# MoBA's output projection in a hybrid decoder layer: y_b kept as pairs of leading bits and rest, products of 512 and 256 columns in place of three of 256, two halves added per block

## The chip, the cores and the metric

The kernel runs on one core of one Trainium2 chip. The metric is the device time of one execution in microseconds (us), the median of a few runs. The profile shown is of one execution of its own.

## The reference, cut to what matters

One decoder layer for 256 tokens of width 1024, all in float32. Two token mixers read the same projection of x, each is projected once more, the two are mixed by gates, and a feed-forward net follows:

```python
proj = jnp.einsum('bsd,dn->bsn', x, w_in)
hq, hf, hi, hg, mq, mk, mv, gate_logits = jnp.split(proj, offsets, axis=-1)
y_a = rms_norm(hgrn2_mixer(hq, hf, hi, lb), hgrn_norm_w) * silu(hg)     # 256 x 1024
y_b = moba_attention(rope(mq), rope(mk), mv)                            # 256 x 1024, 8 heads of 128
z_a = jnp.einsum('bsc,cd->bsd', y_a, w_branch_a)
z_b = jnp.einsum('bsc,cd->bsd', y_b, w_branch_b)                        # the product of this case
g_a, g_b = jnp.split(jax.nn.sigmoid(gate_logits + b_gate), 2, axis=-1)
mixed = jnp.einsum('bsc,cd->bsd', g_a * z_a + g_b * z_b, w_out)
x = layer_norm(DN_ALPHA * x + mixed, ln1_w, ln1_b)
h_gate, h_up = jnp.split(jnp.einsum('bsd,df->bsf', x, w_ffn_in), 2, axis=-1)
y = jnp.einsum('bsf,fd->bsd', silu(h_gate) * h_up, w_ffn_down)
return layer_norm(DN_ALPHA * x + y, ln2_w, ln2_b)
```

With 256 tokens there is one MoBA block, so the attention is plain causal attention over the 256 tokens.

## The kernel before, in words

**Two parts for each operand.** Every float32 operand of a large product is split into its leading bits (`h`, a copy into the type float32r) and the rest (`l`, the difference), `split` at L209. A product a·w is made of three matmuls: h·h, l·h and h·l. Two ways of issuing them matter here:

- `feat_pair` (L298) with `feat_steps` (L349) makes a block of 256 output channels. For each half `f` of 128 channels and each of the eight slices `k` of 128 inputs it issues three matmuls of 256 columns (the tokens): `wh`·`ah` (L353), `wh`·`al` (L354) and `wl`·`ah` (L355). All of them add up in one PSUM tile of 128x512, which holds both halves.
- `wide_pair` (L306) needs the activation as a `Pair` (L166): leading bits and rest of a slice lie side by side in one SBUF tile. For each `f` and `k` it issues one matmul of 512 columns, `wh`·(`ah`,`al`) (L315), and one of 256, `wl`·`ah` (L316). Each half `f` has a PSUM tile (a bank of 128x512) of its own, with the h·h and h·l sums in its first 256 columns and the l part in the last 256. `wide_sum` (L321) then adds the two: for each `f` a ScalarE copy of the last 256 columns to SBUF (L325) and a VectorE add of the first 256 (L326).

The gates `gb` and `ga`, the projection `za` of the other mixer and the feed-forward blocks `fg` and `fu` go by `wide_pair`; the queries and keys and `zb`, the projection of this case, go by `feat_pair`.

**Weights.** `stage` (L217) brings one tile of 128x2048 float32 (1 MB) at a time: SyncE's queue loads it into `raw` (three buffers), ScalarE copies it to `wh` (L236), VectorE subtracts to get `wl` (L238). `wh` and `wl` have four buffers each, so a tile is staged when TensorE has finished with the tile four before. `fetch` (L258) stages up to three tiles ahead of the one that it hands out. Some loads are tied to a transfer on GpSimd's queue that adds up weight blocks in HBM (`sum_weights`, L247); the tiles of `zb` and of `w_out` are not.

**The stretch around the change.** The attention heads (`moba_head`, L696) write their output `po` with `split` into `ybh` and `ybl` (L726), one slice of 256 tokens per head; the eight heads run beside the projections `za0` to `za3` (L754). Then four blocks `zb0` to `zb3` follow (L769): `feat_pair`, the product with the gate on VectorE straight from PSUM (L772), the sum with the other branch (L773), and the split into `mTh` and `mTl` (L774). Slices 2j and 2j+1 of `mTh` and `mTl` come from block j. The products with `w_out` follow (L885 to L917): for the first 128 tokens four groups q = 0 to 3 (`rows_pass`, L783), group q reading slices 2q and 2q+1, 12 matmuls of 512 columns each, in the order `mTh`·`wh`, `mTh`·`wl`, `mTl`·`wh` (L793 to L795); then the layer norm of the first tokens (`norm1(0)`) on VectorE beside the four groups of the second 128 tokens.

**Order.** A scheduler at build time orders the instructions of each engine by its own model of their durations, except inside the stretches marked `manual_schedule`, where TensorE, VectorE and ScalarE follow the order of the program; the products with `w_out` and what follows up to L917 are such a stretch. Each engine then works through its list in that order.

**Memory.** PSUM has eight banks: the pool `mm` (four, used by `za`, `zb` and the attention scores among others) and `aux` (four). At L764 the pools of the scan and the attention (`klp`, `hd2`) are closed, and the pools `late` and `gate` are opened in their place. `kept` is a tile of 128x1024 float32 in `gate`, made at L922 and first written in the feed-forward stage.

Of the kernel before, what the change touches and what calls it, by code (L numbers as in the profile page):

```python
# [10 lines left out]
F32 = mybir.dt.float32  # L11
F32R = mybir.dt.float32r
# [5 lines left out]
P = 128  # L18
T = 256
# [3 lines left out]
H = 8  # L23
# [121 lines left out]
def hybrid_layer_kernel(ctx: ExitStack, tc, x, xw, vecs, wts, ln1_w, ln1_b, ln2_w, ln2_b, consts, out):  # L145
    nc = tc.nc
# [10 lines left out]
    mm = pool("mm", 4, space=PSUM)  # L157
    aux = pool("aux", 4, space=PSUM)

    def slot(name, dt=F32):  # L160
        return big.tile([P, 2048], dt, tag="s8", name=name)

    def r32(ap):
        return ap.bitcast(F32)
# [44 lines left out]
    def split(dst_h, dst_l, src):  # L209
        nc.scalar.copy(dst_h, src)  # L210
        nc.vector.tensor_sub(dst_l, src, r32(dst_h))
# [46 lines left out]
    def fetch(ahead=LOOKAHEAD):  # L258
        while state["next"] < len(loads) and len(ready) < 1 + ahead:
            list(stage())  # L260
        return ready.pop(0)
# [36 lines left out]
    def feat_pair(name, ah=None, al=None, p=mm):  # L298
        ah, al = (xTh, xTl) if ah is None else (ah, al)
        wh, wl = fetch()  # L300
        ps = p.tile([P, 2, T], F32, tag="mm" if p is mm else "aux", name=name)
        for f in range(2):
            feat_steps(ps[:, f, :], wh, wl, f, ah, al, range(KC))
        return ps

    def wide_pair(name, p, tag, a):  # L306


        wh, wl = fetch()
        pss = []  # L310
        for f in range(2):
            ps = p.tile([P, 2, T], F32, tag=tag, name=f"{name}{f}")
            wcol = slice(f * P, (f + 1) * P)
            for k in range(KC):
                nc.tensor.matmul(ps, wh[:, k, wcol], a.both(k), start=(k == 0), stop=False)  # L315
                nc.tensor.matmul(ps[:, 0, :], wl[:, k, wcol], a[0, k, slice(0, T)],  # L316
                                 start=False, stop=(k == KC - 1))
            pss.append(ps)
        return pss

    def wide_sum(pss, dst):  # L321


        for f, z in enumerate(pss):
            nc.scalar.copy(dst[f], z[:, 1, :])  # L325
            nc.vector.tensor_add(dst[f], z[:, 0, :], dst[f])  # L326
# [22 lines left out]
    def feat_steps(ps, wh, wl, f, ah, al, ks, k0=0):  # L349
        wcol = slice(f * P, (f + 1) * P)  # L350
        for k in ks:
            kk = k0 + k
            nc.tensor.matmul(ps, wh[:, k, wcol], ah[:, kk, :], start=(kk == 0), stop=False)  # L353
            nc.tensor.matmul(ps, wh[:, k, wcol], al[:, kk, :], start=False, stop=False)  # L354
            nc.tensor.matmul(ps, wl[:, k, wcol], ah[:, kk, :], start=False, stop=(kk == KC - 1))  # L355
# [81 lines left out]
    for j in range(4):  # L437
        ps = feat_pair(f"hq{j}")
# [5 lines left out]
        for f in range(2):  # L444
            h = 2 * j + f
# [206 lines left out]
    gb = slot("gb").rearrange("p (c t) -> p c t", c=KC)  # L652
# [15 lines left out]
    qT = slot("qT").rearrange("p (h t) -> p h t", h=H)  # L668
    kT = slot("kT").rearrange("p (h t) -> p h t", h=H)
    mv = slot("mv").rearrange("p (t d) -> p t d", t=NT)  # L670
    ybh = slot("ybh", F32R).rearrange("p (h t) -> p h t", h=H)
    ybl = slot("ybl", F32R).rearrange("p (h t) -> p h t", h=H)

    def rope_pair(nm, dst, j, p=mm):
        ps = feat_pair(f"m{nm}{j}", p=p)
# [15 lines left out]
    def spared(i):  # L691
        if not spares:
            spares.append(klp.tile([P, 2, 3 * P], F32, tag="kl", name="ms"))
        return spares[0][:, i, :]

    def moba_head(h):  # L696
        ps = mm.tile([P, 3 * P], F32, tag="mm", name=f"s{h}")
        nc.tensor.matmul(ps[:, 0:P], qT[:, h, 0:P], kT[:, h, 0:P], start=True, stop=True)
        nc.tensor.matmul(ps[:, P:3 * P], qT[:, h, P:T], kT[:, h, :], start=True, stop=True)
        s = hd2.tile([P, 3 * P], F32, tag="ms", name=f"ms{h}") if h % 4 < 2 else spared(h % 4 - 2)  # L700
        st = sm.tile([P, 8], F32, tag="st", bufs=4, name=f"st{h}")
        nc.vector.tensor_tensor(s, ps, causal, op=ALU.add)
        nc.vector.tensor_reduce(st[:, 2:3], s[:, 0:P], axis=mybir.AxisListType.X, op=ALU.max, negate=True)
        nc.vector.tensor_reduce(st[:, 3:4], s[:, P:3 * P], axis=mybir.AxisListType.X, op=ALU.max, negate=True)
        p = s
        nc.scalar.activation(p[:, 0:P], s[:, 0:P], AF.Exp, bias=st[:, 2:3], accum_out=st[:, 4:5])
        nc.scalar.activation(p[:, P:3 * P], s[:, P:3 * P], AF.Exp, bias=st[:, 3:4], accum_out=st[:, 5:6])
        nc.vector.reciprocal(st[:, 6:8], st[:, 4:6])
        nc.scalar.mul(p[:, 0:P], p[:, 0:P], st[:, 6:7])
        nc.scalar.mul(p[:, P:3 * P], p[:, P:3 * P], st[:, 7:8])  # L710
        yield
        pt = aux.tile([P, 3 * P], F32, tag="aux", name=f"pt{h}")
        for b in range(3):
            nc.tensor.transpose(pt[:, b * P:(b + 1) * P], p[:, b * P:(b + 1) * P], ident)
        pT = hd2.tile([P, P], F32, tag="pT", name=f"pT{h}")
        both = hd2.tile([P, 2, T], F32R, tag="sg", bufs=3, name=f"pTp{h}")
        pTh, pTl = both[:, 0, :], both[:, 1, :]
        split(pTh, pTl, pt[:, 0:T])
        nc.scalar.copy(pT, pt[:, T:3 * P])
        hd = slice(h * P, (h + 1) * P)  # L720
        po = aux.tile([P, T], F32, tag="aux", name=f"po{h}")
        nc.tensor.matmul(po, mvh[:, hd], pTh, start=True, stop=False)
        nc.tensor.matmul(po, mvl[:, hd], pTh, start=False, stop=False)
        nc.tensor.matmul(po, mvh[:, hd], pTl, start=False, stop=False)
        nc.tensor.matmul(po[:, P:T], mv[:, 1, hd], pT, start=False, stop=True)
        split(ybh[:, h, :], ybl[:, h, :], po)  # L726
        yield

    def moba_heads():
        heads = [moba_head(h) for h in range(H)]  # L730
        next(heads[0])
        for i in range(H):
            if i < H - 1:
                next(heads[i + 1])
            next(heads[i])
            yield
# [17 lines left out]
    for j in range(4):  # L754
        side.step()
        cs = slice(2 * j, 2 * j + 2)
        if j in PROJECTIONS:
            z = hd2.tile([P, 2, T], F32, tag="sg", bufs=3, name=f"za{j}s")
            wide_sum(wide_pair(f"za{j}", mm, "mm", yP[0]), [z[:, f, :] for f in range(2)])
        else:  # L760
            z = feat_pair(f"za{j}", yah[0], yal[0])
# [4 lines left out]
    gate = pool("gate", 1)  # L766
    mTh = slot("mTh", F32R).rearrange("p (k t) -> p k t", k=KC)
    mTl = slot("mTl", F32R).rearrange("p (k t) -> p k t", k=KC)
    for j in range(4):  # L769
        ps = feat_pair(f"zb{j}", ybh, ybl)  # L770
        cs = slice(2 * j, 2 * j + 2)
        nc.vector.tensor_mul(gb[:, cs, :], ps, gb[:, cs, :])  # L772
        nc.vector.tensor_add(ga[:, cs, :], ga[:, cs, :], gb[:, cs, :])  # L773
        split(mTh[:, cs, :], mTl[:, cs, :], ga[:, cs, :])  # L774

# [143 lines left out]
    e[1][1].transpose()  # L919


    kept = gate.tile([P, 2, 512], F32, tag="kept", name="kept")  # L922
    unit = lambda z: z.rearrange("p (i k t) -> p i k t", i=4, k=KQ // 2)
    spare = []

# [79 lines left out]
    p, f, g = kept[:, 0, :], kept[:, 1, :], room[:, 0, :, :].rearrange("p f t -> p (f t)")  # L1005
# [60 lines left out]
```

## Time and profile before

| | us |
|---|---|
| median of 3 runs | 492.84 |
| the runs | 492.49, 492.84, 805.31 |
| span of the profiled execution | 491.3 |
| median less span | 1.5 |
| TensorE busy in the span | 482.9 (98%) |
| VectorE busy | 396.2 (81%) |
| ScalarE busy | 315.6 (64%) |

The profile gives no device time of its own for the profiled execution, only its span, from the first to the last instruction; 1.5 us is what the median has beside it. PE is TensorE, PEld its weight loads, DVE is VectorE, ACT is ScalarE, POOL is GpSimd, SP is SyncE. A row of the timeline gives start, duration, engine, line, operation, output and input, count, and in brackets how long the engine had been idle and on what it had waited; rows that follow one another directly and are alike are merged into one with a count. L12 is line 12 of the kernel. The duration of a matmul is its time from start to modelled end; one starts before the one ahead of it has ended.

### The profile page before, as it was taken

The page shows a single profiled execution, that of the slowest core. Times are in us where ns is not written, and L with a number is a line of the kernel's source. Part 1 is how long each engine was busy: PE and PEld are TensorE (multiplying, and loading weights), DVE is VectorE, ACT ScalarE, POOL GpSimd, SP SyncE. Part 2 cuts the span into 40 slices and gives each one's busy share as a digit, 9 for nine tenths or more (in the row PEclk, how much of TensorE's full clock was granted, in tenths as well). Part 3 has the DMA queues.
Part 4 walks back from the last instruction along what each step waited for, and adds up shares of the span by engine and source line. Part 5 has one row for each costly group of instructions (what it writes and reads, how often), then busy time and mean ns, then how long its engine had stood idle before and what let it go on. Part 6 is the DMA issues. An engine that isn't in the chain of part 4 may idle for free.

```text
span 491.3 us, 7536 instructions
## 1 busy us (share of the span) xinstructions
PE 482.9 (98%) x2980; PEld 434.0 (88%) x2980; DVE 396.2 (81%) x490; ACT 315.6 (64%) x446; POOL 66.0 (13%) x89
## 2 busy tenths in 40 slices
PE   9999999999999999999999999999999999999994
PEld 9999888888888999999989988888888888898883
DVE  4888899999879869999773999555886779589947
ACT  6797677655879869789762555444565656587700
POOL 2305150530000010010010000001213010000001
PEclk9999999999999999999999999999999999999998
DMA  8879899999996988669776466049999999999702
GB/s 315 371 263 448 273 294 339 316 356 300 343 330 248 318 300 301 229 228 338 255 268 248 177 257 233 18 176 407 286 307 354 317 310 308 297 361 387 257 0 85
DMA packets 25106, 137.79 MB, mean 280 GB/s; under 512 B 2416, under 2 KB 2544, under 8 KB 13424
## 3 DMA queue, kind: packets, MB, share of 16 engines
q1 hardware_dynamic: 15264, 100.63, 53.2%
q0 software_dynamic: 9808, 36.70, 29.0%
q8 instruction: 23, 0.38, 0.3%
q14 instruction: 11, 0.09, 0.0%
HBM read 136.27 MB, written 34.60 MB: 348 GB/s over the span
## 4 chain that ended last, share of the span: by engine, by line
PE 95%; DVE 2%; DMA 2%; issue 0%; ACT 0%; DVEq 0%
PE fu L315 7%; PE fg L315 7%; PE fg L316 3%; PE fu L316 3%; PE gb L315 3%; PE za L315 3%; PE wd L999 2%; PE wd L1000 2%; PE wd L1001 2%; DMA raw<-in_wts_dram 2%; PE sc L514 2%; PE hf L383 2%; PE ga L315 2%; PE hf L384 2%; PE mk L355 2%; PE zb L355 2%
## 5 line engine op out<-in xcount | busy, mean ns | idle before, releaser
L238 DVE TENSOR_TENSOR wl<-raw,wh 128x2048 fp32r<-128x2048 f32 x89 | 203.0, 2289 | 54.0 <-ACT wh L236 53.5
L236 ACT CAST wh<-raw 128x2048 fp32r<-128x2048 f32 x89 | 169.8, 1916 | 73.9 <-PE fg L315 17.6
L315 PE MATMUL fg<-x1p,wh 128*128 128x512 f32 x144 | 50.5, 394 | 0.0
L315 PE MATMUL fu<-x1p,wh 128*128 128x512 f32 x144 | 50.4, 394 | 0.0
L254 POOL TENSOR_TENSOR mark<-ticks 128x1 f32<-128x1 f32 x32 | 24.4, 762 | 180.8 <-DVE ticks L253 159.9
L316 PE MATMUL fg<-x1p,wl 128*128 128x256 f32 x144 | 40.0, 277 | 0.0
L316 PE MATMUL fu<-x1p,wl 128*128 128x256 f32 x144 | 39.9, 277 | 0.0
L315 PEld LDWEIGHTS fu<-x1p,wh 128*128 128x128 f32 x144 | 27.0, 187 | 6.2
L315 PEld LDWEIGHTS fg<-x1p,wh 128*128 128x128 f32 x144 | 27.0, 187 | 6.1
L316 PEld LDWEIGHTS fg<-x1p,wl 128*128 128x128 f32 x144 | 27.0, 188 | 0.1
L316 PEld LDWEIGHTS fu<-x1p,wl 128*128 128x128 f32 x144 | 27.0, 188 | 0.0
L315 PE MATMUL za<-yP,wh 128*128 128x512 f32 x64 | 23.6, 407 | 0.0
L315 PE MATMUL gb<-xP,wh 128*128 128x512 f32 x64 | 22.7, 397 | 0.0
L315 PE MATMUL ga<-xP,wh 128*128 128x512 f32 x64 | 22.6, 396 | 0.0
L256 POOL DMA_DIRECT2D u<-in_wts_dram x24 | 19.7, 827 | 9.7 <-DMA u<-in_wts_dram 7.3
L353 PE MATMUL mq<-xP,wh 128*128 128x256 f32 x64 | 18.6, 291 | 0.0
L354 PE MATMUL mk<-xP,wh 128*128 128x256 f32 x64 | 18.4, 288 | 0.0
L353 PE MATMUL mk<-xP,wh 128*128 128x256 f32 x64 | 18.3, 285 | 0.0
L316 PE MATMUL za<-yP,wl 128*128 128x256 f32 x64 | 18.3, 285 | 0.0
L355 PE MATMUL mq<-xP,wl 128*128 128x256 f32 x64 | 18.2, 284 | 0.0
L355 PE MATMUL mk<-xP,wl 128*128 128x256 f32 x64 | 18.1, 283 | 0.0
L353 PE MATMUL hq<-xP,wh 128*128 128x256 f32 x64 | 18.1, 283 | 0.0
(338 smaller groups left out, 1388.3 us busy)
## 6 DMA issues: line engine op xcount, KB each, us to landing
raw<-in_wts_dram SPq DMA_DIRECT2D x73, 1024.0 KB, 6.3
raw<-u SPq DMA_DIRECT2D x16, 1024.0 KB, 6.7
u<-in_wts_dram POOLq DMA_DIRECT2D x8, 1024.0 KB, 20.5
u<-u POOLq DMA_DIRECT2D x8, 1024.0 KB, 18.2
first<-in_xw_dram SPq DMA_DIRECT2D x6, 640.0 KB, 9.3
xr<-in_x_dram POOLq DMA_DIRECT2D x1, 1024.0 KB, 5.2
wb<-in_ln_w_dram POOLq DMA_DIRECT2D x2, 512.0 KB, 6.6
wb<-in_ln_b_dram POOLq DMA_DIRECT2D x2, 512.0 KB, 7.9
```

The costliest lines, as they stand in the source:

```text
L236: nc.scalar.copy(h[:, ks, :], raw[:, ks, :])
L238: eng.tensor_sub(l[:, ks, :], raw[:, ks, :], r32(h[:, ks, :]))
L254: tc.keep_in_program_order(nc.gpsimd.tensor_tensor(mark, tick, tick, op=ALU.add))
L256: tc.keep_in_program_order(nc.gpsimd.dma_start(source(dst), source(src), **more))
L315: nc.tensor.matmul(ps, wh[:, k, wcol], a.both(k), start=(k == 0), stop=False)
L316: nc.tensor.matmul(ps[:, 0, :], wl[:, k, wcol], a[0, k, slice(0, T)], start=False, stop=(k == KC - 1))
L353: nc.tensor.matmul(ps, wh[:, k, wcol], ah[:, kk, :], start=(kk == 0), stop=False)
L354: nc.tensor.matmul(ps, wh[:, k, wcol], al[:, kk, :], start=False, stop=False)
L355: nc.tensor.matmul(ps, wl[:, k, wcol], ah[:, kk, :], start=False, stop=(kk == KC - 1))
L383: nc.tensor.matmul(pss[f], wh[:, wcol], xTh[:, k, :], start=(k == 0), stop=False)
L384: nc.tensor.matmul(pss[f], wh[:, wcol], xTl[:, k, :], start=False, stop=False)
L514: nc.tensor.matmul(ps[:, a, :], KL[:, h, :], later(Qt, n, h, 1), start=True, stop=True)
```

## The change

`ybh` and `ybl` become the two halves of a `Pair`, so that a head's leading bits and rest lie side by side. The blocks `zb0` to `zb3` are made by `wide_pair`, and `wide_sum` puts the sum of the two halves into one of two halves of `kept`, from which the product with the gate now reads. For that, `kept` is made ahead of the loop and no longer at L922. Weights, their order and the rest of the kernel stay.

```diff
-    ybh = slot("ybh", F32R).rearrange("p (h t) -> p h t", h=H)
-    ybl = slot("ybl", F32R).rearrange("p (h t) -> p h t", h=H)
+    yb = Pair("yb")
+    ybh, ybl = Part(yb, 0), Part(yb, 1)
...
-        split(ybh[:, h, :], ybl[:, h, :], po)
+        split(ybh[:, h, slice(0, T)], ybl[:, h, slice(0, T)], po)
...
+    kept = gate.tile([P, 2, 512], F32, tag="kept", name="kept")
     for j in range(4):
-        ps = feat_pair(f"zb{j}", ybh, ybl)
+        z = kept[:, j % 2, :].rearrange("p (f t) -> p f t", f=2)
+        wide_sum(wide_pair(f"zb{j}", mm, "mm", yb), [z[:, f, :] for f in range(2)])
         cs = slice(2 * j, 2 * j + 2)
-        nc.vector.tensor_mul(gb[:, cs, :], ps, gb[:, cs, :])
+        nc.vector.tensor_mul(gb[:, cs, :], z, gb[:, cs, :])
         nc.vector.tensor_add(ga[:, cs, :], ga[:, cs, :], gb[:, cs, :])
         split(mTh[:, cs, :], mTl[:, cs, :], ga[:, cs, :])
...
-    kept = gate.tile([P, 2, 512], F32, tag="kept", name="kept")
     unit = lambda z: z.rearrange("p (i k t) -> p i k t", i=4, k=KQ // 2)
```

## The prediction

> **What bounds the kernel now.** I read the page first: span, busy shares, chain.
>
> ```profile
> span 491.3 us, 7536 instructions
> ...
> PE 482.9 (98%) x2980; PEld 434.0 (88%) x2980; DVE 396.2 (81%) x490; ACT 315.6 (64%) x446; POOL 66.0 (13%) x89
> ...
> PE 95%; DVE 2%; DMA 2%; issue 0%; ACT 0%; DVEq 0%
> ```
>
> TensorE sets the end: 95% of the chain that ended last is its work. So the question is how much TensorE time the change takes out, and whether the work it puts on VectorE and ScalarE makes TensorE wait. For both I read stretches: first the busy time of each engine in windows around the change (columns: PE, PEld, DVE, ACT, POOL, granted clock, DMA share, GB/s).
>
> ```profile
> 75.00:140.00 65.00, 64.91 (x377) 56.63 (x377) 62.17 (x80) 43.49 (x53) 12.43 (x15) 1.00 1.02 315
> ...
> 259.00:282.61 23.61, 23.61 (x200) 23.61 (x198) 15.65 (x16) 9.31 (x8) 0.00 (x0) 1.00 0.53 203
> ...
> 264.57:270.09 5.52, 5.52 (x48) 5.52 (x47) 0.00 (x2) 0.12 (x1) 0.00 (x0) 1.00 0.45 184
> 270.09:288.18 18.09, 18.09 (x131) 17.13 (x130) 16.66 (x17) 12.09 (x10) 0.00 (x0) 1.00 0.49 178
> ```
>
> The blocks zb0 to zb3 take 23.61 us (second row), TensorE without a gap, clock full. In the 18.09 us that begin with the product for zb0, VectorE is busy for 16.66, so it has 1.43 us left; before that it does nothing for 5.5 us. The first row, where the gates are made by `wide_pair`, is kept for later.
>
> **TensorE's term.** A matmul's duration isn't its price, since starts overlap. The price is the distance of starts. In the timeline, TensorE alone, an unbroken run of zb:
>
> ```profile
> 273.25 0.28 PE L353 MATMUL zb<-ybh,wh 128*128 128x256 f32 x1
> ...
> 282.49 0.28 PE L355 MATMUL zb<-ybh,wl 128*128 128x256 f32 x1
> 282.61 0.40 PE L793 MATMUL wo<-wh,mTh 128*128 128x512 f32 x1
> ```
>
> From 273.25 to 282.61 there are 26 groups of three, 78 matmuls: 9.36 us, 0.120 us each, 0.360 us for a half and a slice. The same for `wide_pair` from the gate gb, an unbroken run of 23 pairs:
>
> ```profile
> 89.82 0.40 PE L315 MATMUL gb<-xP,wh 128*128 128x512 f32 x1
> 90.05 0.28 PE L316 MATMUL gb<-xP,wl 128*128 128x256 f32 x1
> ...
> 97.80 0.39 PE L315 MATMUL gb<-xP,wh 128*128 128x512 f32 x1
> ```
>
> 7.98 us for 23 pairs is 0.347 us for a half and a slice: 0.23 for the 512 columns, 0.117 for the 256. The change removes 192 matmuls of 256 columns and issues 64 of 512 and 64 of 256, with 64 fewer weight loads. The columns streamed are the same. 64 × (0.360 − 0.347) = **0.8 us less** on TensorE.
>
> [...]
>
> **What is added.** For each of the eight halves one ScalarE copy and one VectorE add, as za has them (duration in ns, least/median/most):
>
> ```profile
> L315 PE MATMUL za<-yP,wh x64: 390/395/582, 230.4 to 258.6; 128*128 128x512 f32 x64
> L316 PE MATMUL za<-yP,wl x64: 274/280/368, 230.7 to 258.9; 128*128 128x256 f32 x64
> L325 ACT COPY za0s<-za x2: 393/398/403, 240.1 to 240.4; 128x256 f32<-128x256 f32 x2
> ...
> L326 DVE TENSOR_TENSOR za0s<-za,za0s x2: 415/415/415, 242.6 to 242.9; 128x256 f32<-128x256 f32 x2
> ```
>
> ```profile
> 242.61 0.75 DVE L326 TENSOR_TENSOR za0s<-za,za0s 128x256 f32<-128x256 f32 x2
> ```
>
> ScalarE: 8 × 0.40 = 3.2 us at most, in a stretch where it is busy 9.3 of 23.6 us. VectorE: 8 × 0.415 = 3.3 us, or 2.7 us if they run back to back: the two in the timeline's row take 0.75 us together, so the second adds 0.33. The product with the gate now reads SBUF and not PSUM; elementwise operations of 128x512 on VectorE take 0.68 to 0.69 us in either case (the products and sums of zb in the next fence), so I put that at nothing.
>
> Does this reach TensorE? VectorE's list in the stretch, the part that matters:
>
> ```profile
> 263.89 0.68 DVE L762 TENSOR_TENSOR ga<-za3s,ga 128x512 f32<-128x512 f32 x1
> 270.09 0.69 DVE L772 TENSOR_TENSOR gb<-zb,gb 128x512 f32<-128x512 f32 x1 [5.52 <-PE zb L355]
> 270.82 0.69 DVE L773 TENSOR_TENSOR ga<-ga,gb 128x512 f32<-128x512 f32 x1
> ...
> 281.12 0.69 DVE L773 TENSOR_TENSOR ga<-ga,gb 128x512 f32<-128x512 f32 x1
> 281.73 0.68 DVE L211 TENSOR_TENSOR mTl<-ga,mTh 128x512 fp32r<-128x512 f32 x1
> 282.81 0.69 DVE L772 TENSOR_TENSOR gb<-zb,gb 128x512 f32<-128x512 f32 x1 [0.40 <-PE zb L355]
> 283.54 0.69 DVE L773 TENSOR_TENSOR ga<-ga,gb 128x512 f32<-128x512 f32 x1
> 284.68 2.29 DVE L238 TENSOR_TENSOR wl<-raw,wh 128x2048 fp32r<-128x2048 f32 x1 [0.45 <-ACT wh L236]
> 286.89 1.29 DVE L211 TENSOR_TENSOR mTl<-ga,mTh 128x512 fp32r<-128x512 f32 x2
> 288.09 4.49 DVE L238 TENSOR_TENSOR wl<-raw,wh 128x2048 fp32r<-128x2048 f32 x2
> 292.50 0.68 DVE L804 SCALAR_TENSOR_TENSOR x<-xr,wo 128x512 f32<-128x512 f32 x1
> ```
>
> The first `mTl` of the pair at 286.89 is that of zb2; it ends near 287.6. It stands behind the last w_out tile's `wl`, which itself waits for zb3 to free its `wh` buffer. On TensorE, group q = 2 of the products with w_out needs it here (282.61 + 24 matmuls is the group's start, its third matmul the first reader):
>
> ```profile
> 288.53 0.39 PE L795 MATMUL wo<-wh,mTl 128*128 128x512 f32 x1
> ```
>
> So zb2's rest has 0.9 us to spare, and after the change TensorE wants it 0.8 us earlier, at 287.7. The 5.5 idle us of VectorE before 270.09 don't help if zb0 again ends near 270 (zb0 is held there because its last slice, that of head 7, comes late in the scheduler's order). Then all eight adds fall into the 18.09 us with 1.43 to spare. **Lower bound of the wait: none**, if the scheduler puts zb2's `mTl` ahead of that `wl` of 2.2 us, or zb0 comes earlier. **Upper bound**: 8 × 0.415 = 3.3 us late with none of the 1.43 us used, so 287.6 + 3.3 − 287.7 = 3.2 us. With the same order and the spare used: 2.7 − 1.4 = 1.3 us late, a wait of 1.2 us. I take **0.4 us**, nearer the lower end, because of the first window above: there, with `wide_sum` in the list, VectorE is busy 62.17 of 65 us, as full as here, and TensorE still has 64.91 of 65.
>
> Other edits. The longer chain behind zb3 (a copy of 0.40 and an add of 0.42) is covered: its `mTl` ends at 288.2 and group q = 3 starts 36 matmuls after 282.61, near 290.8; if that cover goes, it costs those 0.8 us. `norm1(0)` at 292.50 follows VectorE's list; what it makes is wanted by the early feed-forward product:
>
> ```profile
> 301.15 2.29 DVE L238 TENSOR_TENSOR wl<-raw,wh 128x2048 fp32r<-128x2048 f32 x1 [0.42 <-ACT wh L236]
> 303.36 1.28 DVE L211 TENSOR_TENSOR x1p<-x1t,x1p 128x512 fp32r<-128x512 f32 x2
> ...
> 305.29 0.39 PE L867 MATMUL fe<-wh,x1p 128*128 128x512 f32 x1
> ```
>
> A VectorE list that is 1.3 us late loses 0.42 at 301.15, and `x1p`, done at 304.64, has 0.65 us before 305.29: 1.1 us of cover, so 0.2 us might show, inside the bounds above. The earlier place of `kept`: its first write must wait until the closed pools' last reader is done, the product on za3 that ends at 264.57. zb0's copies come about 269.6, so it costs nothing; were zb0 earlier (its first half from 262), the copy would stand up to 2.4 us, and ScalarE has nothing else there:
>
> ```profile
> 269.97 1.91 ACT L236 CAST wh<-raw 128x2048 fp32r<-128x2048 f32 x1 [8.26 <-PE zb L354]
> ...
> 282.73 1.91 ACT L236 CAST wh<-raw 128x2048 fp32r<-128x2048 f32 x1 [3.33 <-PE zb L354]
> 284.55 1.13 ACT L210 CAST mTh<-ga 128x512 fp32r<-128x512 f32 x2
> ```
>
> PSUM: a block now takes two `mm` banks, so zb2 waits for zb0's two sums and zb3 for zb1's. A bank is free when copy and add are done, 0.8 us after its last matmul; TensorE meanwhile has the other pair of banks, 16 × 0.347 = 5.6 us of work. At worst the copy stands behind a `wh` of 1.9 us and the add behind a `wl` of 2.3: 5.0 us, still under 5.6, if zb0 doesn't end late against zb1. Cost: nothing, with at most 1 us where zb0 and zb1 end close together. No DMA is added or moved; `Pair` takes two slots, as the two tiles did. Loads follow TensorE's releases and move with it.
>
> **Sum.** −0.8 + 0.4 = −0.4 us: a span of 490.9 after 491.3. The runs have 1.5 us more than this span (492.84): 492.84 − 0.4 = **492.4 us**.
>
> **Rivals.** *VectorE becomes the bound at the seam to w_out (slower).* Its list in 270 to 288 is full, and zb2's `mTl` ends past 287.7, the point from which TensorE waits: 1.2 to 3.2 us, less 0.8: 493.2 to 495.2, taken as 494.5. For it: 1.43 spare us against 2.7 to 3.3 of new work, and two `mTl` already last in the list. Against: the scheduler makes its list anew, and the gates' stretch shows no such wait.
>
> *Matmuls cost their durations (faster).* By those rows of za, a pair costs 395 + 280 = 675 ns, and three zb matmuls of 283 ns cost 849: 64 × 0.174 = 11.1 us, 481.7 us. Against it the starts 0.120 apart: only if three 256-column matmuls really held TensorE 0.85 us could this be, and they hold it 0.36.
>
> [...]
>
> *It changes nothing:* za's interrupted runs and waits eat the 0.8 us, 492.8. This ends within the likeliest case's own spread.
>
> **How the numbers follow.** Forecast (from −0.8 with no wait to no gain): 0.73. VectorE's list makes TensorE wait: 0.19. Durations: 0.01. Overlap: 0.01. The rest, 0.06, is the scheduler reordering more than this stretch, by a few us either way. The two runs near 492.5 differ by 0.35 us; I put three times that below the full gain (492.0) and take the slower rival's upper end: **490.9 to 495.2**. About 2% (9.9 us) is what a measurement of this kernel can tell from no change: faster by more 0.02 (durations, and a share of the rest), slower by more 0.02 (only the rest could), within 0.96.
>
> **What would show it.** Right: 64 rows each of L315 and L316 on zb at 0.35 us a pair, zb from first to last start about 22.8 us and not 23.6; eight copies and adds of 0.4 us; VectorE busy some 3 us more; TensorE without a gap up to w_out's group q = 2 or with less than a microsecond there. Wrong: an `mTl` that TensorE waits for beyond 1 us, gaps between zb1 and zb2 (banks), or L315 on zb closer than 0.2 us to its L316.

## The result, and the profile after

| | before | after |
|---|---|---|
| median, us | 493.06 (6 runs) | 496.82 (6 runs) |
| ratio to before, 95% interval | | 1.0081 (1.0066 to 1.0095) |
| span of the profiled execution, us | 491.3 | 494.1 |

The change makes the kernel 0.8% slower, about 4 us: less than the 2% that the prediction named, but clear of no change by the interval, on the other side of the forecast and above its range. Single executions far above all others (805.31 us of the kernel before here, 2743.74 and 1241.68 us of the layout run and the control below) are left out of the ratios; the medians still count them, and without that one the kernel before has 492.84 us here.

The page of the changed kernel:

```profile
span 494.1 us, 7426 instructions
...
PE 482.7 (98%) x2916; PEld 429.9 (87%) x2916; DVE 398.8 (81%) x498; ACT 317.9 (64%) x454; POOL 64.6 (13%) x89
...
PE 95%; DVE 3%; issue 1%; ACT 1%; DVEq 0%
```

The totals hardly differ: TensorE 482.9 to 482.7, VectorE 2.6 us more. On the chain that ended last VectorE has 3% and not 2%, ScalarE and issue 1% each and not 0%. Two windows of the changed kernel show the place, the first from the first zb matmul to the first product with w_out, the second from there to the first early feed-forward product (columns as in the prediction):

```profile
257.90:281.10 23.20, 23.20 (x136) 20.21 (x134) 15.83 (x20) 11.13 (x15) 0.00 (x0) 1.00 0.56 207
281.10:308.16 27.06, 23.81 (x107) 18.54 (x105) 23.71 (x28) 13.22 (x11) 1.00 (x1) 1.00 0.54 197
```

The same two of the kernel before:

```profile
258.99:282.61 23.62, 23.62 (x200) 23.62 (x198) 15.66 (x16) 9.31 (x8) 0.00 (x0) 1.00 0.53 203
282.61:305.29 22.68, 22.68 (x107) 18.85 (x105) 21.27 (x23) 12.77 (x10) 1.00 (x1) 1.00 0.64 236
```

zb itself is 0.42 us shorter, with TensorE busy throughout. The products with w_out, which the change doesn't touch, are 4.38 us longer, and there TensorE is busy only 23.81 of 27.06 us. So 3.25 us of the 4.38 are idle; in the other 1.1 TensorE counts as busy, but around the two waits shown below its matmuls start 0.33 to 0.39 us apart and not 0.23. The net, 3.96 us, is the whole result: what comes later keeps its length, and the 1.1 us by which zb starts earlier was there before the changed stretch. TensorE in that stretch of the changed kernel:

```profile
287.07 0.40 PE L796 MATMUL wo<-wl,mTh 128*128 128x512 f32 x1
289.21 0.50 PE L797 MATMUL wo<-wh,mTl 128*128 128x512 f32 x1 [1.75 <-DVE mTl L211]
...
291.38 0.39 PE L797 MATMUL wo<-wh,mTl 128*128 128x512 f32 x1
293.27 0.50 PE L795 MATMUL wo<-wh,mTh 128*128 128x512 f32 x1 [1.50 <-ACT mTh L210]
```

It waits twice: in group q = 2 for the rest of zb2 (VectorE), in group q = 3 for the leading bits of zb3 (ScalarE). VectorE's list just before:

```profile
281.55 0.42 DVE L326 TENSOR_TENSOR kept<-zb,kept 128x256 f32<-128x256 f32 x1
281.88 0.68 DVE L774 TENSOR_TENSOR gb<-kept,gb 128x512 f32<-128x512 f32 x1
283.13 2.29 DVE L238 TENSOR_TENSOR wl<-raw,wh 128x2048 fp32r<-128x2048 f32 x1 [0.57 <-ACT wh L236]
285.34 0.69 DVE L775 TENSOR_TENSOR ga<-ga,gb 128x512 f32<-128x512 f32 x1
285.94 2.28 DVE L238 TENSOR_TENSOR wl<-raw,wh 128x2048 fp32r<-128x2048 f32 x1
288.14 0.41 DVE L326 TENSOR_TENSOR kept<-zb,kept 128x256 f32<-128x256 f32 x1
288.48 0.68 DVE L211 TENSOR_TENSOR mTl<-ga,mTh 128x512 fp32r<-128x512 f32 x1
289.07 0.68 DVE L774 TENSOR_TENSOR gb<-kept,gb 128x512 f32<-128x512 f32 x1
289.68 2.28 DVE L238 TENSOR_TENSOR wl<-raw,wh 128x2048 fp32r<-128x2048 f32 x1
291.88 0.68 DVE L775 TENSOR_TENSOR ga<-ga,gb 128x512 f32<-128x512 f32 x1
```

Three splits of weight tiles (L238) now stand among the steps of zb2 and zb3, 2.3 us each. The first is that of the last w_out tile; by the program's names the other two are the first two feed-forward tiles, which nothing wants before 308. In the kernel before those two stood behind the last `mTl`. They belong to the stretch that is ordered by hand; zb3's steps come from the loop ahead of it, and the scheduler put them between instructions of that stretch. zb2's sum (285.34) waits behind one, zb3's second add (288.14) behind two, zb3's sum (291.88) behind three. ScalarE's list has the same fault (in the kernel before, the two weight copies of the feed-forward tiles began at 285.59, behind both `mTh`):

```profile
281.18 3.72 ACT L236 CAST wh<-raw 128x2048 fp32r<-128x2048 f32 x2 [1.90 <-PE zb L315]
284.80 0.36 ACT L325 COPY kept<-zb 128x256 f32<-128x256 f32 x1
286.06 0.62 ACT L210 CAST mTh<-ga 128x512 fp32r<-128x512 f32 x1 [0.89 <-DVE ga L775]
286.58 1.90 ACT L236 CAST wh<-raw 128x2048 fp32r<-128x2048 f32 x1
292.60 0.62 ACT L210 CAST mTh<-ga 128x512 fp32r<-128x512 f32 x1 [4.11 <-DVE ga L775]
```

zb3's last copy could start near 281.3, when its last matmul ends; it starts at 284.80, behind two weight copies.

### The profile page after: what moved, and what is told of

Read it like the earlier page. It is cut to its first block, busy times and chain, and to the rows that moved or that the text cites. A ratio compares the mean times of both kernels' runs of the same rounds, so it can differ in the third digit from the quotient of the medians.

```text
span 494.1 us, 7426 instructions
## 1 busy us (share of the span) xinstructions
PE 482.7 (98%) x2916; PEld 429.9 (87%) x2916; DVE 398.8 (81%) x498; ACT 317.9 (64%) x454; POOL 64.6 (13%) x89
## 4 chain that ended last, share of the span: by engine, by line
PE 95%; DVE 3%; issue 1%; ACT 1%; DVEq 0%
PE fu L315 7%; PE fg L315 7%; PE fg L316 3%; PE fu L316 3%; PE zb L315 3%; PE gb L315 3%; PE za L315 3%; PE ga L315 2%; PE wd L1002 2%; PE wd L1000 2%; PE wd L1001 2%; PE sc L514 2%; PE hq L355 2%; PE hq L354 2%; PE hq L353 2%; PE hf L384 2%
## 5 line engine op out<-in xcount | busy, mean ns | idle before, releaser
L238 DVE TENSOR_TENSOR wl<-raw,wh 128x2048 fp32r<-128x2048 f32 x89 | 203.2, 2288 | 56.9 <-ACT wh L236 56.7
L315 PE MATMUL zb<-yb,wh 128*128 128x512 f32 x64 | 22.8, 399 | 0.0
```

The costliest lines, as they stand in the source:

```text
L238: eng.tensor_sub(l[:, ks, :], raw[:, ks, :], r32(h[:, ks, :]))
```

## The experiments

**Theories.** *Order:* the eight copies and adds cost little themselves, but with them the scheduler makes other lists, in which splits of later weight tiles come ahead of zb2's and zb3's steps. *Volume:* VectorE's list was full, and 3 us more work there come out late in any order. *Layout or matmuls:* the `Pair` of y_b, the place of `kept` or the 512-column matmuls cost.

The measure that serves best is taken from each trace: the time from the first zb matmul to the first product with w_out, from there to the first early feed-forward product (fe), and from there to the first of the wide feed-forward matmuls (fg), in us.

| kernel | zb | w_out | fe to fg | sum | median | ratio (95%) |
|---|---|---|---|---|---|---|
| before | 23.62 | 22.68 | 23.15 | 69.44 | | |
| after | 23.20 | 27.06 | 23.15 | 73.40 | 496.82 | 1.0081 (1.0066 to 1.0095) |
| layout alone | 23.62 | 22.68 | 23.15 | 69.44 | 493.22 | 1.0000 (0.9986 to 1.0015) |
| no copies, no adds | 23.20 | 22.68 | 23.15 | 69.02 | 492.50 | 0.9990 (0.9976 to 1.0003) |
| no adds | 23.20 | 26.18 | 23.15 | 72.52 | 496.48 | 1.0069 (1.0042 to 1.0096) |
| zb3 in the hand-ordered stretch | 23.20 | 22.98 | 23.78 | 69.96 | 494.13 | 1.0021 (1.0006 to 1.0036) |
| the same, one tile later | 23.20 | 22.98 | 23.15 | 69.32 | 492.59 | 0.9997 (0.9988 to 1.0007) |
| before, only the order | 23.62 | 27.57 | 23.15 | 74.34 | 497.88 | 1.0087 (1.0053 to 1.0121) |
| zb0 to zb2 wide, first run | 23.30 | 26.98 | 23.15 | 73.43 | 496.25 (one) | |
| zb0 to zb2 wide, again | 23.30 | 25.38 | 23.15 | 71.83 | 495.63 | 1.0057 (1.0040 to 1.0075) |
| only zb3 wide | 23.51 | 23.65 | 23.15 | 70.30 | 493.06 (one) | |

**Layout alone.** All four blocks made as before, from the `Pair`:

```diff
-        z = kept[:, j % 2, :].rearrange("p (f t) -> p f t", f=2)
-        wide_sum(wide_pair(f"zb{j}", mm, "mm", yb), [z[:, f, :] for f in range(2)])
+        if j in ():
+            z = kept[:, j % 2, :].rearrange("p (f t) -> p f t", f=2)
+            wide_sum(wide_pair(f"zb{j}", mm, "mm", yb), [z[:, f, :] for f in range(2)])
+        else:
+            z = feat_pair(f"zb{j}", ybh, ybl)
```

The condition is never true, so every block goes by the last line.

> Only the Pair layout of y_b and the earlier place of kept stay; all four blocks go back to three matmuls of 256 columns and to the product straight from PSUM. From the first zb matmul to the first matmul of the early feed-forward product there were 46.30 us before and 50.26 after. Order theory (the sums of halves change the lists of VectorE and ScalarE so that later weight tiles are split ahead of zb2's and zb3's chain) and volume theory (eight copies and adds are too much work there, in any order) both say 46.3 us and 493.1 us, no change from before. Layout theory (the pair layout or the place of kept costs): 496 us or more.

Measured 69.44 us in the trace and 493.22 us. Layout and the earlier `kept` cost nothing.

**The matmuls alone, no copies and no adds.**

```diff
-        z = kept[:, j % 2, :].rearrange("p (f t) -> p f t", f=2)
-        wide_sum(wide_pair(f"zb{j}", mm, "mm", yb), [z[:, f, :] for f in range(2)])
         cs = slice(2 * j, 2 * j + 2)
-        nc.vector.tensor_mul(gb[:, cs, :], z, gb[:, cs, :])
+        for f, ps in enumerate(wide_pair(f"zb{j}", mm, "mm", yb)):
+            nc.vector.tensor_mul(gb[:, 2 * j + f, :], ps[:, 0, :], gb[:, 2 * j + f, :])
```

> The wide matmuls alone: no copies, no adds, the product with the gate reads the first 256 columns of each half straight from PSUM (eight products of 128x256 in place of four of 128x512); the part of y_b's rest is missing from the output. Here the last of zb3's chain stands behind one weight tile at most. Order and volume theory: no wait of TensorE, the 0.4 us that zb took less in the changed kernel's trace, 492.7 us. If 512-column matmuls or the PSUM banks cost by themselves: above 494 us.

Measured 492.50 us, 69.02 us in the trace, no wait. In the trace the wide matmuls gain 0.42 us; the interval of the ratio (0.9976 to 1.0003) can't tell that from nothing. Neither they nor the banks cost anything: zb takes as long here, 23.20 us, as in the changed kernel, where copies and adds hold the banks longer. The loss comes with the adding of the halves.

**Copies without the adds.**

```diff
-        wide_sum(wide_pair(f"zb{j}", mm, "mm", yb), [z[:, f, :] for f in range(2)])
+        for f, ps in enumerate(wide_pair(f"zb{j}", mm, "mm", yb)):
+            nc.scalar.copy(z[:, f, :], ps[:, 0, :])
```

> The wide matmuls and eight ScalarE copies stay, the eight VectorE adds are left out: a copy takes the first 256 columns and the part of y_b's rest is missing from the output. In VectorE's list two tiles of the feed-forward weights and the last of w_out still stand ahead of zb3's product and sum. Order theory: TensorE still waits 3 to 4 us in the products with w_out, 495.5 to 496.5 us. Volume theory: with 2.7 to 3.3 us of VectorE work gone the wait is gone too or under 1 us, 492.5 to 493.5 us.

Measured 496.48 us, and TensorE's two waits are there again:

```profile
290.29 0.50 PE L798 MATMUL wo<-wh,mTl 128*128 128x512 f32 x1 [1.70 <-DVE mTl L211]
293.74 0.51 PE L796 MATMUL wo<-wh,mTh 128*128 128x512 f32 x1 [0.85 <-ACT mTh L210]
```

In VectorE's list of this kernel the product of zb3 stands behind two weight splits and its sum behind a third:

```profile
284.54 4.50 DVE L238 TENSOR_TENSOR wl<-raw,wh 128x2048 fp32r<-128x2048 f32 x2 [0.95 <-ACT wh L236]
288.95 0.68 DVE L775 TENSOR_TENSOR gb<-kept,gb 128x512 f32<-128x512 f32 x1
...
290.15 2.29 DVE L238 TENSOR_TENSOR wl<-raw,wh 128x2048 fp32r<-128x2048 f32 x1
292.35 0.69 DVE L776 TENSOR_TENSOR ga<-ga,gb 128x512 f32<-128x512 f32 x1
```

All of VectorE's new work is taken away and TensorE is still 3.1 us late, so the volume on VectorE alone can't be the cause. The eight copies on ScalarE are still there; the next run keeps all of the work and changes its order.

**The full change, zb3 in the hand-ordered stretch.** The loop's body becomes a function `block_b`:

```diff
+    for j in range(3):
+        block_b(j)
...
     with tc.manual_schedule(engines={ET.PE, ET.DVE, ET.Activation}):
+        for j in range(3, 4):
+            block_b(j)
         tiles = [(2 * q,) + fetch(0) for q in range(4)]
```

> The full change with every instruction, but the last block zb3 is put into the hand-ordered stretch of the products with w_out, ahead of them, so that VectorE and ScalarE finish its sums, product, sum and split before they split the last w_out tile and the feed-forward tiles. The volume of work is that of the change. Order theory: no wait in the products with w_out; VectorE then reaches norm1 about 2 us later against TensorE than before, 1.1 of it covered: 46.0 to 47.0 us from first zb to first early product, 492.7 to 493.8 us. Volume theory: TensorE still waits 3 us or more somewhere up to the early product, 496 us or more.

The same instructions, and the products with w_out fall from 27.06 to 22.98 us. VectorE does all of zb3 first and the three weight splits behind it:

```profile
286.76 1.46 DVE L211 TENSOR_TENSOR mTl<-ga,mTh 128x512 fp32r<-128x512 f32 x2
289.35 6.70 DVE L238 TENSOR_TENSOR wl<-raw,wh 128x2048 fp32r<-128x2048 f32 x3 [1.12 <-ACT wh L236]
```

Up to fe it is 46.18 us, inside the order theory's 46.0 to 47.0; the median, 494.13, is 0.3 above its 492.7 to 493.8. The rest of VectorE's lateness shows one step later, as a wait of the early feed-forward product for `x1p` (fe to fg 23.78 in place of 23.15). In this order the added work costs 0.6 us there, and the ratio (1.0006 to 1.0036) stays just above 1; the next run asks whether that is the volume or again the order.

**The same, and one feed-forward tile split behind `x1p`.**

```diff
-            if q < 2:
+            if q == 0:
                 prefetch(1)
+        prefetch(1)
```

> As the run with zb3 in the hand-ordered stretch, and the split of the second of the two feed-forward tiles that stood ahead of x1p's split moved behind it. In that run the early feed-forward product still waited on x1p from VectorE, 0.5 us from first zb to first fg over the kernel before. Order theory: this wait goes, first zb to first fg 69.0 to 69.2 us against 69.45 before and 73.40 after the change, 492.5 us, the gain of 0.3 to 0.4 us on the matmuls. Volume theory: the wait only moves on to the second layer norm and shows there, 69.9 us or more, 493.5 us.

Measured 69.32 us (0.1 above the forecast) and 492.59 us, ratio 0.9997 (0.9988 to 1.0007). Fe to fg is back at 23.15. So the 0.6 us was order as well: the volume is the same. The 0.3 us left in the products with w_out is a wait for the last w_out tile's `wl`. So with a good order the change neither wins nor loses anything that can be measured here, and no version tried beats the kernel before beyond its interval.

**Control: the kernel before with that same move.**

> The kernel before with only that split of a feed-forward tile moved behind x1p's split. Order theory: before had no wait at that place, so nothing changes: 69.4 to 69.5 us from first zb to first fg, 492.9 us. If it gains 0.3 us or more, what the run beside it gains isn't the change's.

Only its times are read, 493.07 us and a ratio of 0.9999 (0.9988 to 1.0010); the 69.4 to 69.5 us of the expectation are not read. By the times, the move alone does nothing.

**The kernel before, only the order changed.** No instruction added; zb3's steps are listed behind the weight tiles, as the changed kernel roughly has them:

```diff
+        if j < 3:
+            chain_b(j, last)
...
         for q in range(4):
+            if q == 3:
+                prefetch(2)
+                chain_b(3, last)
             rows_pass(pss[0], lhs, 0, tiles[q:q + 1], KC)
-        prefetch(2)
```

> The kernel before, with no instruction added or taken away: only zb3's product, sum and split are listed behind the last w_out tile and the first two feed-forward tiles on VectorE and ScalarE, about as in the changed kernel. Order theory: the order alone makes the loss; the product comes near 292 and not 282.8 us, zb3's leading bits near 294.0, and TensorE, which wants them at 290.8, waits 3.2 to 3.5 us: 49.5 to 50.0 us from first zb to first early product against 46.30, 496.1 to 496.6 us. Volume theory: the same work as before, so at most the spare of VectorE is lost, under 1 us, 493.5 us or less.

Measured 497.88 us, 1.0087 (1.0053 to 1.0121): as slow as the change, without any of its work, and 1.3 us above the upper end of the forecast. In the trace VectorE's product for zb3 and TensorE's wait are where they were expected:

```profile
287.87 4.49 DVE L238 TENSOR_TENSOR wl<-raw,wh 128x2048 fp32r<-128x2048 f32 x2
292.28 0.69 DVE L771 TENSOR_TENSOR gb<-zb,gb 128x512 f32<-128x512 f32 x1
```

```profile
290.96 0.39 PE L799 MATMUL wo<-wh,mTl 128*128 128x512 f32 x1
294.39 0.79 PE L797 MATMUL wo<-wh,mTh 128*128 128x512 f32 x1 [3.05 <-ACT mTh L210]
...
295.41 0.63 PE L799 MATMUL wo<-wh,mTl 128*128 128x512 f32 x1
295.84 0.63 PE L797 MATMUL wo<-wh,mTh 128*128 128x512 f32 x1
```

The sum is 1.2 to 1.7 us above the 49.5 to 50.0 expected up to fe (51.19), for a reason that the last two rows show: after the wait the matmuls start 0.43 us apart and not 0.23, at a granted clock of 0.71 (293 to 296) and 0.72 (296 to 299) and not 1.00. The wait itself makes 3.2 us from start to start, of the 4.9 us that the products lose here and against 4.4 us in the changed kernel; the slower starts make the other 1.7. So the order of zb3's steps alone brings back about three quarters of the change's loss as a wait. The wait for zb2's rest isn't in this run, which leaves zb2's steps where they were. The next experiments bear on the slower starts.

**zb0 to zb2 wide, zb3 as before; and only zb3 wide.** (`if j in (0, 1, 2)` and `if j in (3,)` ahead of the wide form, `feat_pair` else.)

> Blocks zb0 to zb2 wide with their sums, zb3 by three matmuls of 256 columns and straight from PSUM. In VectorE's list zb2's product stands behind zb3's, and the last w_out tile and a feed-forward tile ahead of both last splits. Order theory: TensorE waits once, about 2 us, for zb2's split; first zb to first early product 47.7 to 48.5 us against 46.30 before and 50.26 after. Volume theory, each block's two adds a quarter of the loss: three quarters, 49.3 us.

> Only block zb3 wide, zb0 to zb2 by three matmuls of 256 columns. In VectorE's list a w_out tile stands ahead of zb3's second add and a feed-forward tile ahead of its split. Order theory: zb2's split comes in time, zb3's is late by 0.7 us, and some tenths more at x1p: first zb to first early product 46.9 to 47.4 us. Volume theory: a quarter of the loss, 47.3 us; this run doesn't tell the two apart, it shows whether the wait goes to the last group of the products with w_out.

Only zb3 wide: 47.16 us up to fe and one wait of 0.60 us, in the last group, as expected. zb0 to zb2 wide: 50.28 us, 1.8 us above the order theory's upper end and 1.0 above the volume theory's value. The one long wait was the expected one (2.02 us, for zb2's split), but TensorE's clock fell after it:

```profile
287.00:290.00 3.00, 0.89 (x3) 0.30 (x2) 3.00 (x4) 2.02 (x2) 0.00 (x0) 1.00 0.80 309
290.00:293.00 3.00, 2.98 (x10) 2.40 (x11) 2.17 (x1) 0.00 (x0) 0.00 (x0) 0.72 0.95 374
293.00:296.00 3.00, 3.00 (x11) 2.44 (x10) 0.43 (x1) 0.00 (x0) 0.00 (x0) 0.71 0.86 309
```

The third column from the right is the granted clock: 0.72 and 0.71 over two windows. In the timeline nine starts in a row, from 291.28 to 294.92, are 0.28 to 0.43 us apart, seven of them 0.42 to 0.43, in place of 0.23: 1.6 us. The two windows lack 0.28 and 0.29 of 3.00 us each, 1.7 us together; if all of it fell into the 3.36 us from 291.28 to 294.64, the clock there was about half, an estimate from these rows. The next run times the same kernel:

> The kernel with zb0 to zb2 wide once more, timed. In its first execution TensorE's granted clock fell to about half for 3.4 us after a gap of 2.4 us between starts, which was 1.6 us of the loss. If that drop is part of some executions only, the mean clock is near 0.991 in those and 0.995 in the others, which are 1.6 us shorter: 494.6 us. If it comes with every execution: 496.2 us, each at 0.991.

Neither branch came out clean. The spans of its eight executions were 492.6 to 495.3 us; three had a mean clock of 0.993 to 0.994 (spans 494.8, 495.0, 495.3), five had 0.997 to 0.998 (492.6, 493.1, 493.1, 493.4, 494.3). So, by the mean clock, the drop comes in some executions of one and the same kernel, and those are 1.7 us longer on average. The profiled one had no drop (granted clock 1.00 in every window from 278 to 305), the same wait of 2.02 us, and 48.68 us up to fe, 0.2 above the order theory's range.

## Why the prediction was wrong, point by point

- **TensorE's term: right sign, half the size.** 0.8 us was forecast, 0.42 came. A pair of zb costs 23.20/64 = 0.36 us with the other matmuls in that stretch, and 0.353 in unbroken rows, against 0.360 for three of 256. The gb run I chose had 0.347, as the feed-forward blocks have it too (15 pairs at a time at 0.3465), while gb's first stretch had 0.353 and za's unbroken runs 0.348 to 0.372. Why some run 0.006 us slower a pair stays open.
- **"I take 0.4 us" for the wait: the step that failed.** TensorE lost 4.4 us, above even my "upper bound" of 3.2, and the prediction's own sign of being wrong came, an `mTl` that TensorE waits for beyond 1 us (1.75). I had taken VectorE's list of before, added the eight adds to it, and asked how much later its end would come. But the list itself is made anew. The adds and copies are new steps between zb3's last matmul and its split; in the lists that came out, two feed-forward tiles that had stood behind the whole of zb3 stand inside it, and each costs 2.3 us on VectorE and 1.9 on ScalarE. A bound that holds the list fixed is no bound. I did write that the scheduler makes its list anew, but counted it only as a relief, and left its harm to the rest of 0.06. That the order of the lists caused it is shown (same work in another order: gone; no added work, with zb3's steps in the bad order: a wait of 3.05 us); why the scheduler's model prefers this list was not tried.
- **"The gates' stretch shows no such wait": true and beside the point.** There, by the program, no matmul reads what the sums lead to until much later, since the gates are used only with za and zb; at the seam to w_out everything does, within 5.5 us (q = 2) and 8.2 us (q = 3) of zb's last matmul.
- **The slower rival named the right place and a wrong price.** zb2's `mTl` behind the w_out tile's `wl` was there (and a feed-forward tile between them), and the point of waiting was near: 287.7 by my working, and TensorE stood there from 287.3 in a trace whose zb starts 1.1 us earlier, so 288.4 counted as in the kernel before. It priced it by volume, 1.2 to 3.2 us, and left out zb3, which made the second wait of 1.9 us from start to start.
- **ScalarE was costed at nothing** because it is idle for more than half of the stretch. That share says nothing of where the copy stands: zb3's last copy lay 3.5 us behind two weight copies.
- **The cover of the chain behind `norm1` was 2.0 us and not 1.1.** The prediction took the end of both `x1p` splits (304.64), but the first of the two, which ends at 304.04, is enough for the first early products: the weight load that reads it starts at 305.29. That is 1.25 us of room and not 0.65. VectorE's idle time ahead of the splits gave 0.74 us and not 0.42: from the last step of `norm1` to the first `x1p` split it takes 5.80 us before, and 5.06 us in the run with zb3 in the hand-ordered stretch, where no idle time is left. That run agrees with the sum: `norm1` begins 2.95 us later there (12.84 us after the first product with w_out and not 9.89), the products took 0.30 us longer, and 0.63 us showed.
- **Right:** banks (TensorE busy in 23.20 of zb's 23.20 us), layout and `kept` (69.44 us with and without) and the source of the product (0.68 us from SBUF, 0.69 from PSUM) cost nothing; and neither of the two fast outcomes with a chance of 0.01 came: a pair of zb takes 0.353 us in unbroken rows and not 0.675, and in the changed kernel's zb the matmul after one of 512 columns starts 0.23 to 0.24 us behind it (at the least 0.22 in its whole trace); no run shows a closer overlap.
- **The time outside the span** is 1.7 to 2.2 us in the runs that list both, a little more than the 1.5 I used.

## What to carry to other kernels

Where a scheduler lists the instructions, an edit's cost isn't only the work it adds: ask which long, not urgent instructions (here weight splits of 2.3 us) may now be listed ahead of the short ones that the bounding engine waits for, and put one full such instruction, per step of the chain, into the upper bound (a rule drawn from this case and tried on no other). At a seam where the bounding engine needs the result at once, order the chain by hand. A gain of 0.4 us on the matmuls, as here, doesn't pay for sixteen more steps (eight copies, eight adds) on that chain: in the best order tried, 0.1 us of it was left in the trace (69.32 against 69.44) and nothing in the times.

## What the runs showed of the hardware that was not expected

In some executions the matmuls of 512 columns start 0.43 us apart and not 0.23 for some 3 us after a wait of TensorE. Two traces show it. In the first run of zb0 to zb2 wide, after a wait of 2.02 us, the starts stay 0.23 us apart (0.33 the first) until 291.28, 1.3 us after the wait ended; the eight from there to 294.64, in 3.36 us, are 0.37 us apart once and then 0.42 to 0.43. In the order-only kernel, after a wait of 3.05 us, the slow starts are there as the wait ends: seven from 294.39 to 297.54, in 3.15 us, 0.59 us apart once and then 0.42 to 0.43. The granted clock is 0.71 to 0.72 over the windows of 3 us that hold these starts (290 to 296 and 293 to 299). The second trace of zb0 to zb2 wide has the same wait of 2.02 us and no drop, with a granted clock of 1.00. That the wait brings the drop on is the author's reading of these traces; what decides whether it comes, and when it ends, no run shows.

For the other executions only the mean clock and the span speak. Read by these, the drop came in three of eight of zb0 to zb2 wide (mean clocks 0.993 to 0.994), and in three of four of the order-only kernel (0.992, 0.990 and 0.992; the fourth had 0.996 and was 1.6 to 2.8 us shorter in span). The mean clock alone is a weak sign, since one execution of the kernel before has 0.994 as well, at 492.41 us. In the changed kernel, with waits of 1.75 and 1.50 us, the trace has no drop (granted clock 1.00 from 257.90 to 308.16) and all six executions show a mean of 0.995 or 0.996.
